# Input's block sums moved to VectorE and ScalarE, and the sample's new memory computed in the memory's stretch

## The chip, the cores and the metric

One core of one Trainium2 chip. The time is device microseconds of one execution. In what follows PE is TensorE (matmul), PEld its weight loads, DVE is VectorE, ACT is ScalarE, POOL is GpSimd, and SP issues most transfers.

## What is computed

One step of a hybrid encoder layer for 512 frames of a new stream and 32 frames of a running one (T = 544 columns in all, feature rows on the partitions). The input is normalised and projected; then come an mLSTM branch with four heads of 512 and an HGRN2 branch with eight heads of 128, a gated merge and an output block. The part that matters here is the projection and the mLSTM of one head:

```python
xn = _rmsnorm(h, norm_g[l])
proj = xn @ w_in[l]
c = silu(causal_conv(u))
q, k = ch @ w_qm, ch @ w_km * M_HD**-0.5
s = einsum('bhtd,bhsd->bhts', q, k) * dmat
num = w_inter * einsum('bhed,bhtd->bhte', C, q) + einsum('bhts,bhse->bhte', s, v)
den = w_inter * einsum('bhd,bhtd->bht', n, q) + s.sum(-1)
h = num / maximum(abs(den), exp(-m_t))
C_new = decay * C + einsum('bhs,bhse,bhsd->bhed', w_last, v, k)
```

`C_new` is wanted for both streams: the prompt's memory starts from zero, the sample's from a given state.

## The kernel before

Matmuls in full precision are built from two roundings: each operand is a high part (a cast) and a low part (the operand less its high part), and three products are added. Names end in `h` and `l` for the two, and `split_piece` and `weight` (recorded at L128 and L129) make them for weights, the cast on ACT and the subtraction on DVE or POOL. A dense product runs over two column halves of 272.

The order on PE, DVE and ACT is partly written by hand and partly by a scheduler. Start: squares of the input (`r0q`) are added and summed for the norm (`r0pc`, L215), while PE runs the first products `u`; then gates, the four value products `v` (`values`, `values_out` copies them out as `vt`), convolution and SiLU (`cv`, `c`, `cs`). Then for each mLSTM head h: `stage_k` (L149, `k`), `stage_q` in two halves (`q`), for head 0 between them `stage_cols` (gate rows to columns, `cols`) and `stage_decay` (`dm`, from a row `bc` that comes by DMA), `stage_scores` (`sc`, then `dm` times scores, `sh` and `sl`), `mchain`, and `stage_br` (`ya`).

`mchain` is a generator. It transposes and weighs keys (`kt`, then `kwh` on ACT and `kwl` on DVE, L870 and L871; for the sample `kts`, `kws`), transposes values (`vt`, `vh`, `vl`; for the sample `vts`, `vs`), builds the prompt's new memory (`memory`, `C`, `Co`), the numerators with the old state (`nm`, `y`), their statistics (`numbers`), the normalisation (`rs`), the sample's new memory (`Cs`, the last part before `yt`), and after a distance of at least GAP steps the transposes `yt`. Each `yield n` lets a `Pump` run n steps of other work on PE: the remaining projections. These come as `One` (a plain product) or `Two`, which makes two 512-column pieces with seven block products instead of eight (L466 `d`), from sums of weight blocks (`ws`, `wa`) and sums of Input's blocks. PSUM has two double buffers, tag `a` (`paux`), and a ring of four single ones, tag `h` (`phalves` takes two). A `One` or a `Two` holds two of the ring for as long as it runs.

Input's block sums are `xf`. Input has eight row tiles, `xh`/`xl` of 128 x 544. For each pair (k, k + 4) `xf_blocks` adds high and low part into `xr`, and `xf_sums` forms four combinations of the 272-column blocks and splits each into `xfh`, `xfl`. All of it is on POOL, issued in head 0 behind the copy `ksm` (k = 0 to 2) and behind `vsm`. The first `Two` that reads `xfh` is in head 0's `mchain`. POOL is also the engine that makes the first head's key weights' low parts and the copies `r` of gate rows (L692).

The call at the end of `stage_q(0, 1)`, as it stands, and the four calls in `mchain`:

```python
with tc.issue_after(st8[0]["copied"].ins):
    xf_blocks(0)
    xf_sums(0)
    xf_blocks(1)
    xf_blocks(2)
```

Of the kernel before, what the change touches and what calls it, by code (L numbers as in the profile page):

```python
# [33 lines left out]
LEVELS = (1, 2, 4, 8, 16, 32, 64)  # L34
GAP = 16
STEPS = (2, 3, 3, 3, 3, 3, 3)
# [17 lines left out]
WSPLIT = 256  # L54
U5, U7, U6, U4 = range(4)
TAIL = (5, 4)
# [6 lines left out]
def hybrid_step(ctx: ExitStack, tc: tile.TileContext, a, o):  # L63
# [238 lines left out]
    one, other = half(0), half(1)  # L302
    xraw = {}

    def xf_blocks(k):

        if k < KD // 2 - 1:
            t = xp.tile([P, 2 * T], F32, tag="x0", name=f"xr{k}")
            x = t[:, :T], t[:, T:]
        else:  # L310
            x = slot(f"xr{k}0")[:, :T], slot(f"xr{k}1")[:, :T]
        for t, i in zip(x, (k, k + KD // 2)):
            G.tensor_tensor(t, xs[i][0].bitcast(F32), xs[i][1].bitcast(F32), ALU.add)
        xraw[k] = x

    def xf_sums(k):

        x1, x2 = xraw[k]
        u = cp.tile([P, T], F32, tag="lm", name=f"xu{k}")
        u5, u7 = u[:, :TH], u[:, TH:T]  # L320
# [4 lines left out]
        def part_of(src, n):  # L325
            G.tensor_copy(h[:, n], src)
            G.tensor_tensor(l[:, n], src, h[:, n].bitcast(F32), ALU.subtract)

        G.tensor_tensor(u5, x1[:, one], x1[:, other], ALU.subtract)
        part_of(u5, U5)  # L330
        G.tensor_tensor(u7, x2[:, other], x1[:, other], ALU.subtract)
        part_of(u7, U7)
        G.tensor_tensor(x1[:, one], x1[:, one], x2[:, other], ALU.add)
        G.tensor_tensor(x2[:, other], x1[:, other], x1[:, one], ALU.subtract)
        G.tensor_tensor(x1[:, other], x1[:, other], x2[:, one], ALU.add)
        G.tensor_tensor(x2[:, one], x1[:, one], x1[:, other], ALU.subtract)
        part_of(x2[:, one], U4)
        part_of(x2[:, other], U6)
        xf.append((h, l))

    xf = []

# [373 lines left out]
    def stage_decay(h):  # L716

        bc = tp.tile([P, T + NS], F32, tag="bc", name=f"bc{h}")
        nc.sync.dma_start(bc, nm_d[h : h + 1, :].to_broadcast([P, T + NS]))
        d01 = [slot(f"dm{h}0"), slot(f"dm{h}1")]  # L720
        d2 = slot(f"dm{h}2")
        dj = [d01[0][:, 0:512], d01[1][:, 0:384], d2[:, 0:256], d2[:, 256:384]]
        ds = d2[: 3 * NS, 384 : 384 + NS]
        for j in range(NB):
            V.tensor_tensor(dj[j][:, :P], bc[:, NS + j * P : NS + (j + 1) * P], cmask, ALU.add)
# [6 lines left out]
        S.activation(ds, ds, AF.Exp, bias=cols[:, 0, h : h + 1])  # L732
        wi = cp.tile([P, NS], F32, name=f"wi{h}")
        G.tensor_copy(wi, bc[:, T : T + NS])
        st8[h].update(dj=dj, ds=ds, wi=wi)

# [51 lines left out]
    def stage_scores(h):  # L788
# [9 lines left out]
        for j in range(NB):  # L798
# [16 lines left out]
            S.copy(sh, dj[j])  # L815
            V.tensor_tensor(sl, dj[j], sh.bitcast(F32), ALU.subtract)
            st.append((sh, sl))
# [12 lines left out]
        V.tensor_tensor(dss[2 * NS :], ds[2 * NS :], dss[2 * NS :].bitcast(F32), ALU.subtract)  # L830
        st8[h].update(st=st, dss=dss)

    def memory(h, f, kw, vv, pool=paux):
# [23 lines left out]
    def mchain(h, pump):  # L857

        t = st8[h]

        kf, ksm = t["kf"], t["ksm"]
        kw = []
# [56 lines left out]
        lo = slice(NS, 2 * NS)  # L919
        V.tensor_tensor(vs[lo, :HD], pt[lo, 0, :], vs[lo, :HD].bitcast(F32), ALU.subtract)  # L920
# [20 lines left out]
        st, dss, qw, wi = (t[k] for k in ("st", "dss", "qw", "wi"))  # L941
        stt = small("stat", [P, NB + 1, 2])
# [42 lines left out]
        for i in range(NB):  # L985
# [15 lines left out]
            numbers(i, P, y)  # L1001
            yb.append(y)
        yb.append(ysm)
        n5 = NB + 1
        with tc.high_priority():
# [11 lines left out]
            for i in range(n5):  # L1017
# [4 lines left out]
                else:  # L1022
                    V.tensor_scalar(y, y, stt[:p, i, 0:1], rs[:p, i : i + 1], ALU.subtract, ALU.mult)

        for f in range(KH):
            yield 1
            pn = paux(f"Cs{h}{f}")
            for g in range(2):
                PE.matmul(
                    pn[:, g, :VH],  # L1030
                    kws[:, f * P : (f + 1) * P],
                    vs[:, g * VH : (g + 1) * VH],
                    start=True,
                    stop=True,
                )
            V.scalar_tensor_tensor(
                two(c0[f][:, :VW]), two(c0[f][:, :VW]), wi[:, NS - 1 : NS], pn[:, :, :VH], ALU.mult, ALU.add
            )
            nc.sync.dma_start(o["Cs"][h, f], c0[f][:, :VW])


# [18 lines left out]
    def stage_br(h):  # L1060

        hs = st8[h]["hs"]
        for u in range(4):
# [12 lines left out]
            if h + 1 < MH and len(st8[h + 1]["cc"]) < KH:  # L1076
                conv(h + 1)
        st8[h].clear()

    def level_masks():  # L1080
# [13 lines left out]
    with tc.manual_schedule(engines={mybir.EngineType.Activation, mybir.EngineType.DVE, mybir.EngineType.PE}):  # L1094
# [15 lines left out]
        for k in range(KD):  # L1110
# [10 lines left out]
            sqk = slot(f"r0q{k}")[:, :T]  # L1121
            if k in (1, 3, 5, 6, 7):
                S.activation(sqk, t[:, :T], AF.Square)
            else:
                G.tensor_tensor(sqk, t[:, :T], t[:, :T], ALU.mult)
            sq.append(sqk)
            if k in (1, 3, 5):
                G.tensor_tensor(sq[k - 1], sq[k - 1], sqk, ALU.add)
            if k > 1:
                products(k - 2)  # L1130
        for i, j in ((6, 7), (0, 2), (4, 6), (0, 4)):
            V.tensor_tensor(sq[i], sq[i], sq[j], ALU.add)
# [83 lines left out]

        values()
        conv_rest(0, uin[0], cv[0])
        silu()
        next(gates)  # L1220
        values_out()
        values()
        for f in range(1, KH):
            conv_rest(f, uin[f], cv[f])
            silu_low(f - 1)
            silu()
            if f == 1:
                values_out()
                values()
        values_out()  # L1230
        values()
        silu_low(KH - 1)
        for _ in range(GATED):
            next(gates)
    with tc.manual_schedule(engines={mybir.EngineType.PE}):
        for h in range(MH):
# [8 lines left out]
            if h == 0:  # L1245

                st8[0]["wq"] = weight(a["w_qm"][0, 0], "wq00")
                high, low = made["wq001"]
                with tc.issue_after(high.ins), tc.issue_after(low.ins):
                    *_, (nm_d, *rows) = gates  # L1250

                    lb, lc = cp.tile([P, HH], F32, name="lb"), cp.tile([P, HH], F32, name="lc")
                    l0, l1 = vec[:, V_LB : V_LB + HH], vec[:, V_LB + HH : V_LB + 2 * HH]
                    lm, le = small("lbm", [P, HH]), small("lbe", [P, 2, HH])
                    V.tensor_tensor(lm, l0, l1, ALU.max)
                    V.tensor_tensor(le[:, 0, :], l0, lm, ALU.subtract)
                    V.tensor_tensor(le[:, 1, :], l1, lm, ALU.subtract)
                    S.activation(le, le, AF.Exp)
                    V.tensor_tensor(lm, le[:, 0, :], le[:, 1, :], ALU.add)
                    V.reciprocal(lm, lm)  # L1260
                    V.tensor_tensor(lb, le[:, 0, :], lm, ALU.mult)
                    V.tensor_tensor(lc, le[:, 1, :], lm, ALU.mult)
            stage_q(h, 0)
            if h == 0:
                col, cols, combo = stage_cols(*rows)
                stage_decay(h)
            low = stage_q(h, 1)
            if h == 0:
                pump.behind = low
                with tc.issue_after(st8[0]["copied"].ins):  # L1270
                    xf_blocks(0)
                    xf_sums(0)
                    xf_blocks(1)
                    xf_blocks(2)
            else:
                pump = Pump(fill(h))
                pump.to(2)
            stage_scores(h)
            pump.run(mchain(h, pump))
            pump.end()  # L1280
            if h < MH - 1:
                stage_br(h)
            if h == 0:
                lmask = level_masks()
    nc.scalar.dma_start(o["u"], uo)
# [445 lines left out]
```

## Time and profile before

| | us |
|---|---|
| median of 3 runs | 1204.21 (1203.91 to 1205.76) |
| profiled execution | 1204.12 |
| its span | 1202.4 |
| mean granted PE clock | 0.989 |
| busy: PE, DVE, ACT, POOL | 1164.4, 887.8, 611.1, 188.0 |

Two views carry most of what follows. A row of the waits gives the waiting engine, tile and line, what it waited for, the total, the number of times and the longest. A row of a timeline gives start, duration, engine, line, operation, tiles and sizes, and in brackets the idle time before and what ended it; x2 means two instructions in one row, and the duration is then that of both. A line number such as L149 or L129 is that of a helper that many stages use, so the tiles tell which stage it is.

### The profile page before, as it was taken

What the parts mean: (1) busy time and instruction counts of PE and PEld (TensorE: products, weight loads), DVE (VectorE), ACT (ScalarE), POOL (GpSimd) and SP (SyncE); (2) the same over time, 40 slices, a digit from 0 to 9 for tenths busy, and PEclk for the clock granted to TensorE, in tenths of its full rate; (3) what the DMA queues carried; (4) which work ended last, traced back from release to release, by engine and by line L of the source; (5) the groups of instructions that cost most, each with busy time, mean ns of one, the idle gap of its engine ahead of it and who ended that gap; (6) DMA issues with size and microseconds to landing.
All of it is one profiled execution on the core that took longest, in us unless ns stands there. A gap on an engine that the chain in (4) does not pass through costs nothing.

```text
span 1202.4 us, 24275 instructions
## 1 busy us (share of the span) xinstructions
PE 1164.4 (97%) x9089; PEld 1133.9 (94%) x9089; DVE 887.8 (74%) x2099; ACT 611.1 (51%) x1344; POOL 188.0 (16%) x349
## 2 busy tenths in 40 slices
PE   9986898999999999999999999999999999999998
PEld 8985888999989999899999999999999999999998
DVE  7876768568598685986887577777778998654485
ACT  5673435746465564665564244434334566533462
POOL 5938541010010110001100011110011100000000
PEclk9996999999999999999999999999999999999999
DMA  6132211513255132552556321212222263322653
GB/s 225 55 101 78 71 71 61 182 53 133 80 155 187 54 116 84 164 176 73 183 173 209 108 69 60 69 62 69 67 62 77 67 219 96 120 89 84 222 183 111
DMA packets 77902, 135.82 MB, mean 113 GB/s; under 512 B 8788, under 2 KB 16340, under 8 KB 77784
## 3 DMA queue, kind: packets, MB, share of 16 engines
q1 hardware_dynamic: 77616, 134.21, 34.3%
q8 instruction: 71, 1.16, 0.4%
q14 instruction: 47, 0.39, 0.1%
q10 hardware_dynamic: 168, 0.06, 0.0%
HBM read 109.32 MB, written 24.91 MB: 112 GB/s over the span
## 4 chain that ended last, share of the span: by engine, by line
PE 85%; DVE 6%; ACT 3%; POOL 3%; issue 2%; DMA 0%; SPq 0%; ACTq 0%; DVEq 0%; POOLq 0%
PE d L466 21%; PE d L379 17%; PE ya L149 8%; PE pg L1590 4%; PE yb L149 4%; PE o L149 4%; PE k L149 4%; PE C L840 4%; PE q L149 4%; PE sc L803 2%; PE pl L1386 2%; PE nm L992 2%; DVE cv L580 1%; PE u L269 1%; PE ple L149 1%
## 5 line engine op out<-in xcount | busy, mean ns | idle before, releaser
L1378 ACT COPY km<-hk 128x256 f32<-128x256 f32 x56 | 24.0, 428 | 81.9 <-DVE hk L1404 61.1
L580 DVE SCALAR_TENSOR_TENSOR cv<-ub,vec,cv 128x547 f32<-128x547 f32 x48 | 40.1, 835 | 0.5
L1440 POOL TENSOR_TENSOR at<-at,tri 32x32 f32<-32x32 f32 x8 | 3.8, 472 | 208.7 <-DVE at L1411 208.7
L1386 PE MATMUL pl<-hq,km 128*128 128x128 f32 x224 | 35.9, 284 | 0.0
L892 DVE TENSOR_TENSOR c0l<-c,c0h 128x516 fp32r<-128x516 f32 x16 | 13.3, 852 | 26.2 <-ACT c0h L891 26.1
L1404 DVE TENSOR_TENSOR hq<-hq,q 128x128 f32<-128x128 f32 (+1 forms) x96 | 25.3, 294 | 9.7 <-PE pl L1386 8.4
L479 ACT COPY t<-d 128x272 f32<-128x272 f32 x78 | 29.4, 377 | 2.9 <-DVE ub L487 2.6
L1386 PEld LDWEIGHTS pl<-hq,km 128*128 128x128 f32 x224 | 30.8, 191 | 0.0
L851 ACT COPY Co<-C 128x258 f32<-128x258 f32 x32 | 10.4, 378 | 33.6 <-PE C L840 33.6
L1404 DVE TENSOR_TENSOR hk<-hk,q 128x128 f32<-128x128 f32 x96 | 26.2, 286 | 0.2
L1409 DVE COPY_PREDICATED at<-lmask,pl 128x256 f32<-128x256 uint8 x56 | 24.8, 443 | 0.0
L1074 DVE TENSOR_TENSOR y<-ya,y 128x272 f32<-128x272 f32 x48 | 18.9, 435 | 7.9 <-PE ya L149 7.9
L1328 POOL TENSOR_TENSOR kq<-q,hk 128x544 f32<-128x544 f32 x8 | 13.9, 1733 | 60.5 <-DVE q L1326 57.6
L1500 ACT ACTIVATE osq<-kq 128x128 f32<-128x128 f32 x32 | 9.9, 311 | 25.5 <-DVE kq L1494 24.8
L953 DVE BATCH_NORM_STATS2 bs<-y 128x6 f32<-128x512 f32 (+1 forms) x20 | 13.7, 685 | 10.9 <-ACT y L1000 10.8
L742 POOL COPY vsm<-vt 128x96 f32<-128x96 f32 x16 | 7.6, 483 | 87.1 <-ACT vt L489 43.6
L573 POOL COPY uo<-ub 128x3 f32<-128x3 f32 x16 | 9.2, 573 | 71.7 <-DVE ub L485 37.8
L1000 ACT COPY y<-nm 128x516 f32<-128x516 f32 x16 | 9.4, 589 | 20.5 <-PE nm L992 14.8
L840 PE MATMUL C<-vh,kwh 128*128 128x258 f32 x96 | 19.4, 284 | 0.0
L840 PE MATMUL C<-vl,kwh 128*128 128x258 f32 x96 | 19.4, 284 | 0.0
L840 PE MATMUL C<-vh,kwl 128*128 128x258 f32 x96 | 19.3, 283 | 0.0
L992 PE MATMUL nm<-vh,sh 128*128 128x258 f32 x80 | 16.5, 288 | 2.7 <-ACT y L1000 2.5
(4087 smaller groups left out, 4925.9 us busy)
## 6 DMA issues: line engine op xcount, KB each, us to landing
ya_d<-y SPq DMA_DIRECT2D x32, 272.0 KB, 2.4
y<-ya_d SPq DMA_DIRECT2D x24, 272.0 KB, 4.3
c<-in_C SPq DMA_DIRECT2D x16, 258.0 KB, 3.4
out_Cp<-Co SPq DMA_DIRECT2D x16, 258.0 KB, 2.4
out_Cs<-c SPq DMA_DIRECT2D x16, 258.0 KB, 2.8
x<-in_xT SPq DMA_DIRECT2D x8, 272.5 KB, 4.7
ya<-ya_d SPq DMA_DIRECT2D x8, 272.0 KB, 5.1
h<-in_xT SPq DMA_DIRECT2D x8, 272.0 KB, 3.7
```

The costliest lines, as they stand in the source:

```text
L149: PE.matmul(both[b][:m, :TH], part(w, off + k * step, m, x), xx[:, half(b)], start=(k == 0 and j == 0), stop=(k == n - 1 and j == 2),)
L379: PE.matmul(self.ps[b][:, : c.stop - c.start], part(self.w, k * P, P, x), xx[:, c], start=(k == 0 and j == 0), stop=(k == KD - 1 and j == 2),)
L466: PE.matmul(ps, ww[:, c], xx, start=(start and k == 0 and j == 0), stop=end, skip_group_check=not start,)
L479: S.copy(t, ps)
L580: V.scalar_tensor_tensor(cv[:, :547], ub[:, j : j + 547], vcol(V_CW + 4 * ft + j), cv[:, :547], ALU.mult, ALU.add)
L803: PE.matmul(pn[:, 0, :n], ks[f][x][:, j * P : (j + 1) * P], qs[f][y][:, NS + j * P : T], start=(f == 0 and i == 0), stop=(f == KH - 1 and ...
L840: PE.matmul(pn[g][:, :VH], kw[b][x][:, f * P : (f + 1) * P], vv[b][y][:, g * VH : (g + 1) * VH], start=(b == 0 and j == 0), stop=(b == NB ...
L992: PE.matmul(pn[:, g, :VH], st[j][x][:, (i - j) * P : (i - j + 1) * P], vv[j][y][:, g * VH : (g + 1) * VH], start=(j == 0 and q == 0), stop ...
L1386: PE.matmul(pn[:, 0, b * P : (b + 1) * P], km[:, b * P : (b + 1) * P], view(qq, b * P, ((2 * c, P // (2 * c)), (HB + c, 2), (1, c))), star ...
L1404: V.tensor_tensor(xv[:, :, i, :], xv[:, :, i, :], t[:, :, 1 - i : 2 - i].to_broadcast([P, m, c]), ALU.mult)
L1409: V.copy_predicated(at[:, :NA], lmask[:, li, :NA], pn[:, 0, :NA])
L1590: PE.matmul(ps, part(w, k * P, P, x), xx[:, c], start=(k == 0 and j == 0), stop=(k == KD - 1 and j == 2))
```

## The change

Block sums. `xf_blocks` is gone. `xf_sums` does ten operations on DVE and three on ACT: it adds high and low part (544 columns for the first tile, two halves for the second), forms the four combinations in place with four more, casts on ACT and subtracts on DVE. Two of the combinations are cast and split together as 544 columns; the fourth comes out with its sign changed, which the multiplication by −1 undoes. k = 0 and 3 are issued behind the last low part of the scores, k = 1 and 2 behind the low part of `vs`. U4 and U6, which number the combinations, swap places. Scratch is the `lm` tile and the three `half` tiles that `Two` uses as well.

The sample's memory. `new_memory(f)` replaces the last loop before `yt`. It takes single halves of the ring instead of a double buffer, so that DVE has two additions of 258 columns per f instead of one of 516. It is called behind `memory(f)` for f = 0, 1 and behind the numerators 1 and 2 for f = 2, 3; in the last head behind each numerator. The loop's four `yield 1` go, and GAP is 20 instead of 16, so `yt` stands at the same distance.

Smaller parts: the level masks are issued behind the last weight split of `stage_br(0)`; HGRN2's lower bounds are computed in three places (start, behind the decays, behind the scores); the gate rows' POOL and DVE work is bound behind `wk011`'s low part; ACT squares all input tiles but two, and DVE adds two pairs early and three at the end; `values` and `values_out` are issued earlier.

```diff
-GAP = 16
+GAP = 20
-U5, U7, U6, U4 = range(4)
+U5, U7, U4, U6 = range(4)
...
     def xf_sums(k):
...
+        x11, x12 = u[:, one], u[:, other]
+        x21, x22 = (tp.tile([P, TH], F32, tag="half", name=f"xv{k}{b}", bufs=3) for b in range(2))
+        (h1, l1), (h2, l2) = ([t.bitcast(F32) for t in xs[i]] for i in (k, k + KD // 2))
+        V.tensor_tensor(u, h1, l1, ALU.add)
+        for b, t in enumerate((x21, x22)):
+            V.tensor_tensor(t, h2[:, half(b)], l2[:, half(b)], ALU.add)
+        V.tensor_tensor(x11, x11, x12, ALU.subtract)
+        V.tensor_tensor(x12, x22, x12, ALU.subtract)
+        V.tensor_tensor(x22, x11, x22, ALU.add)
+        V.tensor_tensor(x21, x22, x21, ALU.subtract)
+        S.copy(h[:, :2], two(u))
+        V.tensor_tensor(l[:, :2], two(u), h[:, :2].bitcast(F32), ALU.subtract)
+        S.copy(h[:, 2], x21)
+        V.tensor_tensor(l[:, 2], x21, h[:, 2].bitcast(F32), ALU.subtract)
+        S.mul(h[:, 3], x22, -1.0)
+        V.scalar_tensor_tensor(l[:, 3], x22, -1.0, h[:, 3].bitcast(F32), ALU.mult, ALU.subtract)
+        return h, l
...
         if h == 0:
-            with tc.issue_after(copied.ins):
-                xf_sums(1)
-                xf_sums(2)
-                xf_blocks(3)
-                xf_sums(3)
+            with tc.issue_after(low.ins):
+                for k in (1, 2):
+                    xf[k] = xf_sums(k)
...
+        def new_memory(f):
+
+            pn = phalves(f"Cs{h}{f}")
+            for g in range(2):
+                v = slice(g * VH, (g + 1) * VH)
+                PE.matmul(pn[g][:, :VH], kws[:, f * P : (f + 1) * P], vs[:, v], start=True, stop=True)
+                V.scalar_tensor_tensor(c0[f][:, v], c0[f][:, v], wi[:, NS - 1 : NS], pn[g][:, :VH], ALU.mult, ALU.add)
+            nc.sync.dma_start(o["Cs"][h, f], c0[f][:, :VW])
...
                 for _ in memory(h, f, kw, vv):
                     pass
+                if f < 2:
+                    new_memory(f)
...
             yb.append(y)
+            if h == MH - 1:
+                new_memory(i)
+            elif i in (1, 2):
+                new_memory(i + 1)
...
-        for f in range(KH):
-            yield 1
-            pn = paux(f"Cs{h}{f}")
...
-            if k in (1, 3, 5, 6, 7):
+            if k not in (0, 2):
                 S.activation(sqk, t[:, :T], AF.Square)
...
-            if k in (1, 3, 5):
+            if k in (1, 3):
                 G.tensor_tensor(sq[k - 1], sq[k - 1], sqk, ALU.add)
+            if k in (5, 6):
+                i, j = ((0, 2), (4, 5))[k - 5]
+                V.tensor_tensor(sq[i], sq[i], sq[j], ALU.add)
...
-        for i, j in ((6, 7), (0, 2), (4, 6), (0, 4)):
+        for i, j in ((0, 4), (6, 7), (0, 6)):
...
-                high, low = made["wq001"]
-                with tc.issue_after(high.ins), tc.issue_after(low.ins):
+                with tc.issue_after(made["wq001"][0].ins), tc.issue_after(made["wk011"][1].ins):
                     *_, (nm_d, *rows) = gates
...
-                with tc.issue_after(st8[0]["copied"].ins):
-                    xf_blocks(0)
...
-            stage_scores(h)
+            low = stage_scores(h)
+            if h == 0:
+                with tc.issue_after(low.ins):
+                    for k in (0, 3):
+                        xf[k] = xf_sums(k)
+                    lower_bounds()
...
             if h == 0:
-                lmask = level_masks()
+                with tc.issue_after(last.ins):
+                    lmask = level_masks()
```

How the order of instructions moves, at three places (numbers behind tile names are buffer numbers). First, DVE in head 0's q stage, before and then after; `wq010l` and `wq011l` are the low parts of the second query weight, `dm` the start of the decay matrices, line 725 before and 712 after.

```order
L707 COPY col<-cols 128x72
L709 COPY cols<-cols 96x12
L129 TENSOR_TENSOR wq010l<-wq01r_1398,wq010h 128x512
L725 TENSOR_TENSOR dm_1377<-bc_1375,cmask 128x128
L725 TENSOR_TENSOR dm_1378<-bc_1375,cmask 128x128
L725 TENSOR_TENSOR dm_1379<-bc_1375,cmask 128x128 x2
L726 TENSOR_TENSOR dm_1379<-bc_1375,cmask_128 96x32
L129 TENSOR_TENSOR wq011l<-wq01r_1400,wq011h 128x512
```

```order
L694 COPY col<-cols 128x72
L696 COPY cols<-cols 96x12
L129 TENSOR_TENSOR wq010l<-wq01r_1394,wq010h 128x512
L129 TENSOR_TENSOR wq011l<-wq01r_1396,wq011h 128x512
L712 TENSOR_TENSOR dm_1367<-bc_1365,cmask 128x128
```

The second low part has moved ahead of the five `dm` operations; on POOL the operations of the sums that stood between the last `ksm` copy and the `vsm` copies are gone, and so are those behind them. Second, DVE in head 0 behind the scores, after the change: `xu` and `xv` are scratch of the sums, `xfl` their low parts, `lbm`, `lb`, `lc` the lower bounds. These are the first of the four `kwl` and the rows behind it.

```order
L859 SCALAR_TENSOR_TENSOR kwl_1621<-kt_1615,col,kwh_1620 128x512
L318 TENSOR_TENSOR xv_1571<-xu_1569,xv_1571 128x272
L1080 RECIPROCAL lbm<-lbm 128x8
L319 TENSOR_TENSOR xv_1570<-xv_1571,xv_1570 128x272
L321 TENSOR_TENSOR xfl_1568<-xu_1569,xfh_1567 128x544
L323 TENSOR_TENSOR xfl_1568<-xv_1570,xfh_1567 128x272
L325 SCALAR_TENSOR_TENSOR xfl_1568<-xv_1571,xfh_1567 128x272
L313 TENSOR_TENSOR xu_1587<-xh_604,xl_605 128x544
L315 TENSOR_TENSOR xv_1589<-xh_628,xl_629 128x272
L316 TENSOR_TENSOR xu_1587<-xu_1587 128x272
L1081 TENSOR_TENSOR lb<-lbe,lbm 128x8
L1082 TENSOR_TENSOR lc<-lbe,lbm 128x8
```

One more operation of the sums (L317) and then the second `kwl` follow. Before, these two `kwl` stood next to each other (L871). Ahead of the first `kwl` now stand six operations of the sums (L313 to L317) that before were on POOL. Third, PE in head 1, around the sample's memory of f = 0, after the change: `C` is the prompt's memory, `Cs` the sample's.

```order
L828 MATMUL C_3968<-vh_3879,kwl_3645 128x258 x2
L921 MATMUL Cs_3997<-vs,kws 128x258
L921 MATMUL Cs_3998<-vs,kws 128x258
L828 MATMUL C_4004<-vh_3821,kwh_3492 128x258 x2
L828 MATMUL C_4004<-vl_3822,kwh_3492 128x258 x2
```

Before, `C` of f = 0 was followed at once by `C` of f = 1, and the four pairs of `Cs` came behind all numerators with six matmuls of `d` between two pairs. The second `Cs` here takes the one half of the ring that the first has left to DVE.

More of the change, by code (lines that the diff above doesn't have):

```diff
@@ L302, in hybrid_step @@
     one, other = half(0), half(1)
[L303 to L314, printed above, removed]
     def xf_sums(k):
-        x1, x2 = xraw[k]
-        u = cp.tile([P, T], F32, tag="lm", name=f"xu{k}")
-        u5, u7 = u[:, :TH], u[:, TH:T]
         ring = f"x{int(k in (1, 2))}"
@@ L323, in xf_sums @@
         l = xp.tile([P, 4, TH], F32R, tag=ring, name=f"xfl{k}")
[L325 to L341, printed above, removed]
+        u = cp.tile([P, T], F32, tag="lm", name=f"xu{k}")
+        x11, x12 = u[:, one], u[:, other]
[15 more added lines that the diff above has]
+        return h, l
+    xf = [None] * (KD // 2)
     class One:
@@ L815, in stage_scores @@
             S.copy(sh, dj[j])
-            V.tensor_tensor(sl, dj[j], sh.bitcast(F32), ALU.subtract)
+            low = V.tensor_tensor(sl, dj[j], sh.bitcast(F32), ALU.subtract)
             st.append((sh, sl))
@@ L831, in stage_scores @@
         st8[h].update(st=st, dss=dss)
+        return low
     def memory(h, f, kw, vv, pool=paux):
@@ L859, in mchain @@
         t = st8[h]
-        kf, ksm = t["kf"], t["ksm"]
+        kf, ksm, wi = t["kf"], t["ksm"], t["wi"]
         kw = []
@@ L938, in mchain @@
                     pass
-        st, dss, qw, wi = (t[k] for k in ("st", "dss", "qw", "wi"))
+                if f < 2:
+                    new_memory(f)
+        st, dss, qw = (t[k] for k in ("st", "dss", "qw"))
         stt = small("stat", [P, NB + 1, 2])
@@ L1023, in mchain @@
                     V.tensor_scalar(y, y, stt[:p, i, 0:1], rs[:p, i : i + 1], ALU.subtract, ALU.mult)
-        for f in range(KH):
-            yield 1
-            pn = paux(f"Cs{h}{f}")
[L1028 to L1039, printed above, removed]
         hs = []
@@ L1078, in stage_br, with hgrn_bounds, rest @@
         st8[h].clear()
+        return made[f"wbm{h}31"][1]
+    lb, lc = cp.tile([P, HH], F32, name="lb"), cp.tile([P, HH], F32, name="lc")
+    def hgrn_bounds(decayed):
+        l0, l1 = vec[:, V_LB : V_LB + HH], vec[:, V_LB + HH : V_LB + 2 * HH]
+        lm, le = small("lbm", [P, HH]), small("lbe", [P, 2, HH])
+        V.tensor_tensor(lm, l0, l1, ALU.max)
+        V.tensor_tensor(le[:, 0, :], l0, lm, ALU.subtract)
+        V.tensor_tensor(le[:, 1, :], l1, lm, ALU.subtract)
+        with tc.issue_after(decayed.ins):
+            S.activation(le, le, AF.Exp)
+        def rest():
+            V.tensor_tensor(lm, le[:, 0, :], le[:, 1, :], ALU.add)
+            V.reciprocal(lm, lm)
+            V.tensor_tensor(lb, le[:, 0, :], lm, ALU.mult)
+            V.tensor_tensor(lc, le[:, 1, :], lm, ALU.mult)
+        return rest
     def level_masks():
@@ L1217, in hybrid_step @@
         values()
+        values_out()
+        values()
         conv_rest(0, uin[0], cv[0])
@@ L1225, in hybrid_step @@
             silu_low(f - 1)
+            if f == KH - 1:
+                values_out()
+                values()
             silu()
@@ L1281, in hybrid_step @@
             if h < MH - 1:
-                stage_br(h)
+                last = stage_br(h)
             if h == 0:
-                lmask = level_masks()
+                with tc.issue_after(last.ins):
+                    lmask = level_masks()
     nc.scalar.dma_start(o["u"], uo)
```

25 lines of the change are left out of this document (4 added, 21 removed).

## The prediction

> **What bounds the kernel now.** I read the busy times first, then the whole list of what TensorE waited for, then the stretches in which it waits. The page's busy row of each engine:
>
> ```profile
> span 1202.4 us, 24275 instructions
> PE 1164.4 (97%) x9089; PEld 1133.9 (94%) x9089; DVE 887.8 (74%) x2099; ACT 611.1 (51%) x1344; POOL 188.0 (16%) x349
> ```
>
> TensorE (PE) is the bound: 38.0 us of the span are not matmul, and only those, and matmuls that run slowly, can be won. The profiled execution took 1204.12 us, 1.7 us more than its span, and agrees with the median of 1204.21 us, so I work from 1204.1. The view of PE's waits (total us, times, longest) has nearly all of the 38 us; these are the rows that the change can touch:
>
> ```profile
> PE d L466 <- DVE ub L485: 6.0, 3, 3.0
> PE q L149 <- DVE wq010l L129: 5.4, 1, 5.4
> PE q L149 <- DVE wq011l L129: 4.7, 1, 4.7
> PE nm L992 <- ACT y L1000: 2.5, 1, 2.5
> PE vts L915 <- POOL vh L908: 2.0, 1, 2.0
> PE cols L705 <- POOL r L692: 1.9, 1, 1.9
> PE k L149 <- POOL wk001l L129: 1.7, 1, 1.7
> PE d L379 <- ACT vt L1201: 1.5, 1, 1.5
> PE r0pc L215 <- DVE r0q L1132: 1.3, 1, 1.3
> PE d L466 <- ACT t L479: 1.2, 1, 1.2
> PE kt L867 <- DVE dm L810: 1.2, 1, 1.2
> PE v L149 <- DVE vt L1203: 1.0, 1, 1.0
> PE Cs L1029 <- DVE c L1036: 0.3, 1, 0.3
> ```
>
> Two of them, in head 0's q stage, are 10.1 us. The table by stretches shows what goes on there (columns: length, then busy us of PE, PEld, DVE, ACT and POOL with counts, then the granted PE clock):
>
> ```profile
> 20.00:30.00 10.00, 8.72 (x58) 8.38 (x57) 6.72 (x27) 1.48 (x6) 0.00 (x0) 0.83 0.32 106
> 90.00:100.00 10.00, 7.66 (x64) 7.09 (x63) 5.04 (x12) 6.17 (x21) 9.98 (x15) 0.86 0.47 155
> 100.00:110.00 10.00, 3.09 (x12) 2.76 (x12) 10.00 (x4) 1.57 (x5) 10.00 (x16) 0.50 0.08 26
> 110.00:120.00 10.00, 7.24 (x36) 7.07 (x37) 4.33 (x10) 3.55 (x12) 6.50 (x18) 0.61 0.16 58
> 280.00:320.00 40.00, 39.95 (x328) 39.51 (x327) 25.96 (x47) 20.15 (x43) 2.13 (x9) 1.00 0.31 107
> ```
>
> From 100 to 110 DVE began only 4 instructions, with POOL busy without a gap, and PE's clock was 0.50. The timelines of DVE and POOL have the instructions (start, duration):
>
> ```profile
> 98.66 6.32 DVE L129 TENSOR_TENSOR wq010l<-wq01r,wq010h 128x512 fp32r<-128x512 f32 x1
> 104.90 6.55 DVE L725 TENSOR_TENSOR dm<-bc,cmask 128x128 f32<-128x128 f32 x4
> 112.03 0.68 DVE L129 TENSOR_TENSOR wq011l<-wq01r,wq011h 128x512 fp32r<-128x512 f32 x1
> ```
>
> ```profile
> 100.00 1.32 POOL L313 TENSOR_TENSOR xr<-xh,xl 128x544 f32<-128x544 f32 x1
> ```
>
> The same operation took 6.32 us in one place and 0.68 us, once POOL was quieter, 13 us later. POOL was doing Input's block sums there (`xr`, `xu`, `xfh`, `xfl`), which began behind the `ksm` copies. [...]
>
> **The change, part by part.**
>
> *The q stage: about −15.7 us.* These are PE's rows at the stage's start, its last pair of matmuls, and the first of the scores behind it:
>
> ```profile
> 98.07 0.32 PE L705 MATMUL cols<-ident,r 4*96 4x4 f32 x2 [1.94 <-POOL r L692]
> 118.83 0.42 PE L149 MATMUL q<-cs3h,wq011l 128*128 128x272 f32 x2
> 119.08 0.63 PE L803 MATMUL sc<-q,kh 128*128 128x512 f32 x2
> ```
>
> From 98.32 to 119.08 are 20.76 us for 48 matmuls. Two take 0.25 us (118.83 to 119.08), so 6.0 us would do; 5.4 and 4.7 us are the two waits, and the remaining 4.7 us is a slow clock (0.50 and 0.61 in the table). In the new order POOL has no sums there, `r` no longer stands behind any, and DVE makes `wq010l` and `wq011l` one behind the other, ahead of `dm`. PE gets `cols` 1.94 us sooner; then DVE copies `cols` (0.3 us) and makes `wq010l` (0.68), while PE needs that after its first four matmuls (0.5): 0.5 us of waiting is left, and `wq011l` is ready before its turn. Gain 1.94 + 5.4 + 4.7 + 4.7 − 0.5 = 16.2; I take 15.7, leaving 0.5 for matmuls that still run slowly after the small `cols` ones. Bounds: 12.5 (3 us of slow clock stay) to 16.5. The scores need `q`'s low parts and `dm`, each then short on a free DVE: nothing later there that I can find.
>
> *From the start to k: about −4.5 us.* Gone are the wait at `r0pc` (1.3; three additions of squares at the end instead of four, and no POOL squares beside DVE), at `v` (1.0) and `vt` (1.5), since `values_out` is issued earlier, and at `wk001l` (1.7, as POOL no longer copies `r` first): 5.5 us. The clock of 0.83 from 20 to 30, 10 × 0.17 = 1.7 us, may go with the first. What is late next is ScalarE's cast of the first key weight, with POOL's low part behind it:
>
> ```profile
> 72.99 0.61 ACT L128 CAST wk000h<-wk00r 128x512 fp32r<-128x512 f32 x1
> 73.67 1.32 POOL L129 TENSOR_TENSOR wk000l<-wk00r,wk000h 128x512 fp32r<-128x512 f32 x1 [12.51 <-ACT wk000h L128]
> 74.63 0.41 PE L149 MATMUL k<-cs0h,wk000h 128*128 128x272 f32 x2
> ```
>
> The cast ended 1.0 us before PE used it, and now two `vt` copies (0.6 us) stand ahead of it. The chain before it (convolution, SiLU, two function tables) moves forward too, by the shift at `rb` and by two DVE operations fewer ahead of the last convolution, but not by all of PE's 5 us. I charge 2.5 us at `wk000h` and `wk000l`: 5.5 + 1.7 − 2.5 = 4.7, rounded to 4.5. Bounds: 2.0 to 7.2.
>
> *Head 0 from scores to normalise: about +1.1 us.* Gone: `kt` 1.2, `vts` 2.0, `nm` 2.5, `t` 1.2 and `Cs` 0.3, all with POOL's sums at their source: 7.2. New: the sums of k = 0 and 3 stand in DVE's queue before and between the four `kwl`. The prices of their operations, and of `kwl`, from rows on a DVE that was not held up:
>
> ```profile
> 120.05 0.79 DVE L780 TENSOR_TENSOR q<-q,q 128x272 fp32r<-128x272 f32 x2 [4.00 <-ACT q L779]
> 130.92 0.75 DVE L871 SCALAR_TENSOR_TENSOR kwl<-kt,col,kwh 128x512 fp32r<-128x512 f32 x1
> 192.87 0.73 DVE L102 TENSOR_TENSOR hm0l<-c,hm0h 128x544 fp32r<-128x544 f32 x1
> ```
>
> One sum has two operations of 0.73 and eight of 0.40 us, 4.7 us. PE's transposes `kt` have two buffers, each freed by a `kwl`, and between two of them PE has about 1.2 us of other work. Six operations stand ahead of the first `kwl`, 0.73 + 5 × 0.40 = 2.7 us: a wait of 1.5. Nine and three tiny ones of the bounds stand ahead of the second; DVE starts them closer than they last, so about 4.0 us, and with `kwl` itself, less PE's work, a wait of 3.5. What stands before the third and fourth makes `vt` wait 0.8 and `vts` 1.2. Together 7.0, and a slow clock behind the longest. That one I price by a wait of the same length:
>
> ```profile
> 203.57 0.59 PE L466 MATMUL d<-xfh,ws16h 128*128 128x272 f32 x1 [2.99 <-DVE ub L485]
> 203.96 0.43 PE L466 MATMUL d<-xfl,ws16h 128*128 128x272 f32 x1
> ```
>
> The 12 matmuls behind it took 0.23 us each instead of 0.125: 1.3 us. The sums of k = 1 and 2 (9.4 us of DVE) lie beside the memory's matmuls and are not needed until `d` some 20 us later; I cost them at nothing. Without that cover they would cost up to 9.4 us. Sum: 7.0 + 1.3 − 7.2 = +1.1. Bounds: −3 (ScalarE's copies of the sums let `kwl` pass sooner) to +10.
>
> *The sample's memory, heads 1 to 3: about +7.8 us.* `Cs` now takes single halves of PSUM. In head 0 two halves are free. From head 1 on two seven-product units hold three of four, so the second half's matmul waits until DVE has added the first from PSUM. No row of before has this wait; its parts have:
>
> ```profile
> 172.47 0.75 DVE L1036 SCALAR_TENSOR_TENSOR c<-c,wi,Cs 128x516 f32<-128x516 f32 x1
> 173.27 0.51 PE L1029 MATMUL Cs<-vs,kws 96*128 96x258 f32 x2 [0.26 <-DVE c L1036]
> 189.53 0.43 DVE L487 SCALAR_TENSOR_TENSOR ub<-d,t 128x272 f32<-128x272 f32 x1
> 200.30 0.29 PE L466 MATMUL d<-xfh,ws36l 128*128 128x272 f32 x1
> ```
>
> The matmul takes 0.29 us to its end, the addition of 258 columns about 0.43, and PE went on 0.05 us after such a release (172.47 + 0.75 = 173.22, start 173.27); less the 0.12 us that it would have run anyhow, 0.65 us. Four f in three heads make 12 such waits: 7.8 us. Bounds: 0.35 us each, 4 us (if the rows overstate the matmul's end), to 1.2 each, 14 us (one `BATCH_NORM_STATS` or split of 0.7 us ahead on DVE). DVE is busy 25.96 of 40 us in the head's quiet part (280 to 320). Behind each addition on DVE wait only splits for later units.
>
> *Heads 1 and 2 behind the normalise: about −2.4 us.* Two of the three `ub` waits (1.5 each) are theirs. In the new order DVE has two splits (0.6 each) behind it before `yt` that stood after it, so I take 1.2 off each; bounds 0 and 3.6. Head 0's wait of 3.0 with its slow clock I leave, since the order there is the same. The lower bounds, the level masks (now where DVE has room) and the swapped order of two blocks I cost at 0 within ±1.
>
> Sum: −15.7 − 4.5 + 1.1 + 7.8 − 2.4 = −13.7, so **1190 us**.
>
> **The rivals.**
>
> *DVE becomes the bound of head 0.* All four sums add 18.8 us to DVE from 120 to 165. For it: they are 18.8 us more in 45 us where it already waits in line. Against: most of them have PE work beside them. If k = 1 and 2 are not hidden, 9.4 us come on top: about 1199.
>
> *The long `ub` wait goes too.* With 3.0 + 1.3 us in head 0, the rest of the 3.6 in heads 1 and 2, and the start at its best: 1190 − 4.3 − 1.2 − 2 = about 1183. For it: the masks and additions leave DVE ahead of that wait. Against: its chain starts at `yt`.
>
> *The hand-over in halves eats everything.* All else gives 21.5 us (13.7 + 7.8), so 12 hand-overs must cost over 1.8 us each to make the kernel slower. That needs three operations ahead of each addition on DVE; the 3.0 us of `ub` shows PE held by such a queue, and at 3.0 each the time is 1204.1 − 21.5 + 36 = 1219. Against: the additions stand next to each other in the new order, with DVE a third idle.
>
> *The hand-over lowers the clock.* If each short gap brought the 1.3 us of slow matmuls seen after 203.57, that is 15.6 us more: about 1205, no change. Against: after waits of 1.0 and 1.5 us (`v`, `vt`) no slow stretch follows. [...]
>
> That POOL's sums did not hold up DVE at all, and 6.32 us came from elsewhere, I give no chance of its own: it would leave the q stage as it is.
>
> **How the numbers follow.** Forecast 1190: 0.60; DVE bound in head 0, 1199: 0.16; `ub` wait gone, 1183: 0.14; clock, 1205: 0.04; slow hand-over, 1219: 0.06. A measurement of this kernel tells about 0.2%, 2.4 us, from no change. So faster 0.90, same 0.04, slower 0.06. The range 1181 to 1200 holds the first three and leaves out the last two with the tails of the others.
>
> **What would show it.** Right: `wq010l` at 0.7 us, the clock at 1.00 between 90 and 110, and in the waits a row of `Cs` on DVE with 12 times and about 8 us; in head 0 a row of `kt` on `kwl` of about 5 us. Wrong: `Cs` waits over 1 us each, a lower clock in the memory's stretches, waits of `d` on `xfl`, or a k stage that starts no earlier.

## The result, and the profile after

| | before | after |
|---|---|---|
| median of 17 runs each, us | 1203.12 (1201.25 to 1205.76) | 1200.46 (1197.59 to 1204.94) |
| ratio, 95% interval | | 0.9981 [0.9971, 0.9991] |
| profiled execution, us | 1204.12 | 1202.97 |

2.7 us came of a forecast 13.7. The profiled execution of after is 2.5 us above its median. First the page's busy row, then the waits of PE:

```profile
span 1201.3 us, 24295 instructions
PE 1170.1 (97%) x9089; PEld 1138.1 (95%) x9089; DVE 885.6 (74%) x2156; ACT 615.7 (51%) x1357; POOL 133.7 (11%) x283
```

```profile
PE Cs L921 <- DVE c L922: 8.9, 12, 2.6
PE kt L855 <- DVE kwl L859: 4.8, 2, 3.3
PE d L453 <- DVE ub L472: 3.1, 1, 3.1
PE d L453 <- ACT wbm101h L128: 1.6, 1, 1.6
PE d L453 <- ACT wbm201h L128: 1.6, 1, 1.6
PE v L149 <- ACT vt L1210: 1.5, 1, 1.5
PE k L149 <- POOL wk000l L129: 1.3, 1, 1.3
PE vts L903 <- DVE vl L895: 1.1, 1, 1.1
PE q L149 <- DVE wq010l L129: 0.3, 1, 0.3
```

Span less PE's busy time fell from 38.0 to 31.2 us, 6.8 us, but PE was busy 5.7 us longer with as many matmuls. The mean clock hardly differs (0.991 against 0.989), but before's longest slow stretch lay beside waits (100 to 120), while those of after lie where PE works. The q stage's 10.1 us of waits are down to 0.3; the `Cs` row has the forecast 12 times. The table by stretches (columns as in the prediction):

```profile
20.00:30.00 10.00, 9.62 (x76) 9.10 (x75) 6.71 (x29) 2.53 (x10) 0.57 (x1) 1.00 0.33 114
60.00:80.00 20.00, 18.51 (x133) 18.06 (x133) 17.01 (x29) 14.68 (x28) 5.31 (x4) 0.91 0.34 105
90.00:100.00 10.00, 9.70 (x87) 9.32 (x86) 5.23 (x18) 7.51 (x27) 2.06 (x9) 1.00 0.51 165
100.00:110.00 10.00, 10.00 (x71) 9.45 (x71) 8.30 (x17) 5.32 (x12) 3.44 (x10) 1.00 0.36 111
280.00:320.00 40.00, 37.67 (x299) 36.46 (x298) 24.94 (x71) 19.43 (x41) 1.26 (x9) 1.00 0.25 84
600.00:620.00 20.00, 18.21 (x120) 17.38 (x121) 10.94 (x40) 6.50 (x12) 0.00 (x0) 0.83 0.16 59
```

From 90 to 110 the clock is full, as forecast. From 280 to 320, in head 1's memory, PE is idle 2.3 us at a full clock: four hand-overs (the matmul of one half, its addition on DVE, then the matmul that reuses the half). From 600 to 620, in the last head's memory, the clock is 0.83: 20 × 0.17 = 3.4 us. PE's timeline shows a hand-over in head 1 and the first in the last head:

```profile
286.93 0.28 PE L921 MATMUL Cs<-vs,kws 96*128 96x258 f32 x1
287.79 0.39 PE L921 MATMUL Cs<-vs,kws 96*128 96x258 f32 x1 [0.58 <-DVE c L922]
...
597.18 0.28 PE L921 MATMUL Cs<-vs,kws 96*128 96x258 f32 x1
600.06 0.39 PE L921 MATMUL Cs<-vs,kws 96*128 96x258 f32 x1 [2.60 <-DVE c L922]
...
601.23 0.63 PE L990 MATMUL nm<-vh,sh 128*128 128x258 f32 x2
601.66 0.63 PE L990 MATMUL nm<-vl,sh 128*128 128x258 f32 x2
...
610.93 0.40 PE L990 MATMUL nm<-vh,sh 128*128 128x258 f32 x2
611.17 0.40 PE L990 MATMUL nm<-vl,sh 128*128 128x258 f32 x2
```

The second matmul starts 0.86 us behind the first in head 1, 0.74 more than the 0.12 without a wait. Eleven of the twelve waits are such ones of 0.58. The twelfth is 2.60, and behind it a pair of matmuls takes 0.43 us instead of 0.24 until 607.3. DVE's timeline shows why:

```profile
597.67 0.68 DVE L129 TENSOR_TENSOR ws346l<-ws,ws346h 128x512 fp32r<-128x512 f32 x1
598.27 0.69 DVE L880 TENSOR_TENSOR c0l<-c,c0h 128x516 fp32r<-128x516 f32 x1
598.87 0.69 DVE L951 BATCH_NORM_STATS2 bs<-y 128x6 f32<-128x512 f32 x1
599.48 0.14 DVE L953 COPY den<-y 128x1 f32<-128x1 f32 x1
599.53 0.47 DVE L922 SCALAR_TENSOR_TENSOR c<-c,wi,Cs 128x258 f32<-128x258 f32 x1
```

The first matmul of the two ended at 597.46, and four operations stood ahead of its addition.

### The profile page after: what moved, and what is told of

Read it like the earlier page. It is cut to its first block, busy times and chain, and to the rows that moved or that the text cites. A ratio compares the mean times of both kernels' runs of the same rounds, so it can differ in the third digit from the quotient of the medians.

```text
span 1201.3 us, 24295 instructions
## 1 busy us (share of the span) xinstructions
PE 1170.1 (97%) x9089; PEld 1138.1 (95%) x9089; DVE 885.6 (74%) x2156; ACT 615.7 (51%) x1357; POOL 133.7 (11%) x283
## 5 line engine op out<-in xcount | busy, mean ns | idle before, releaser
L922 DVE SCALAR_TENSOR_TENSOR c<-c,wi,Cs 128x258 f32<-128x258 f32 x32 | 15.2, 480 | 19.1 <-PE Cs L921 19.0
L921 PE MATMUL Cs<-vs,kws 96*128 96x258 f32 x32 | 10.2, 336 | 8.9 <-DVE c L922 8.9
L742 ACT ACTIVATE kf<-k 128x272 f32<-128x272 f32 x32 | 10.9, 392 | 14.6 <-PE k L149 14.6
L573 ACT ACTIVATE c<-cv 128x32 f32<-128x32 f32 x16 | 3.7, 230 | 27.8 <-DVE cv L567 27.8
```

## The experiments

**Theory A** after the result: the block sums brought what was forecast, and the hand-over took it back, much of it in the last head. **Theory C**, for the rest: the start brought 1 to 2.5 us, not 4.5.

**The sample's memory back as it was** (after, with before's loop over `f` and its GAP):

```diff
-GAP = 20
+GAP = 16
...
-                if f < 2:
-                    new_memory(f)
...
-            if h == MH - 1:
-                new_memory(i)
-            elif i in (1, 2):
-                new_memory(i + 1)
...
+        for f in range(KH):
+            yield 1
+            pn = paux(f"Cs{h}{f}")
...
```

> The changed kernel with the sample's memory put back where it was (a double buffer per f, behind the normalise, distance 16); all else as changed. Theory A (the hand-over of single halves, with what follows it, costs some 14 us in heads 1 to 3: 12 waits of 0.58 or more, the late first one in the last head, and the slow clock behind two of them): about 1188, 12 us under the changed kernel, no row of Cs on DVE over 0.3 us in the waits. Rival B (the gain of head 0 is lost again to a clock that falls somewhere else whenever a wait goes, whatever is done with the sample's memory): within 3 us of the changed kernel, 1198 to 1203.

1188.14 us against 1203.94 of before on that chip, ratio 0.9869 [0.9854, 0.9884]. So all the rest of the change brings 15.8 us, and the sample's memory in its new place costs 1200.46 − 1188.14 = 12.3. Its waits have no row of `Cs`. The three `ub` waits stay:

```profile
PE d L453 <- DVE ub L472: 6.1, 3, 3.1
PE kt L855 <- DVE kwl L859: 4.8, 2, 3.3
```

**The sample's memory alone, on before** (GAP 20, `new_memory` and its calls; nothing else of the change):

> The kernel before with the sample's memory alone moved and cut into halves, as in the change. Theory A: 10 to 15 us slower than before, 1213 to 1218, with 12 waits of Cs on DVE, about 9 us, and the rest as slow clock and matmul tails. Rival B: within 3 us of before.

1220.95 us, ratio 1.0146 [1.0121, 1.017]: 17 us slower than before, more than expected and more than the 12.3 it costs in after. Two waits more than in after, in head 0 (5.4 and 0.5 us), are somewhat more than the difference of 4.7; the row of the waits, then DVE's timeline before the longest:

```profile
PE Cs L935 <- DVE c L936: 14.8, 14, 5.4
```

```profile
163.25 0.83 DVE L1083 TENSOR_SCALAR lmask<-sxt 128x256 uint8<-128x256 f32 x1 [2.84 <-POOL xfl L327]
...
168.01 0.47 DVE L936 SCALAR_TENSOR_TENSOR c<-c,wi,Cs 128x258 f32<-128x258 f32 x1
```

The level masks, which reuse a buffer of POOL's block sums, wait for these at 163.25 and stand ahead of the addition until 168.01. In after they are elsewhere, and head 0 has no such wait: the parts of the change lean on each other.

**Block sums alone, on before** (the new `xf_sums`, its calls and the order of U4 and U6):

> The kernel before with the block sums alone moved to VectorE and ScalarE. If it is POOL's sums that held DVE up in the q stage: wq010l at 0.7 us instead of 6.32, and 11 to 15 us faster than before (1188 to 1192), a little less than with wq011l moved ahead of dm as well, and the waits of kt on kwl of about 5 us appear. Rival (the order of wq011l behind dm, or the r copies, carry most of the q stage): under 6 us faster, wq011l or cols still waited for 3 us or more.

1189.26 us, ratio 0.9878 [0.9863, 0.9892]: 1203.94 − 1189.26 = 14.7 us. `wq010l` lasts 0.68 us, and PE waits 0.3 for it and 0.8 for `wq011l`. For `kwl` it waits 1.5 at `kt` and 2.1 at `kts`, 3.6 of the expected 5.

**The start alone, on before**:

```diff
-            if k in (1, 3, 5, 6, 7):
+            if k not in (0, 2):
                 S.activation(sqk, t[:, :T], AF.Square)
...
+            if f == KH - 1:
+                values_out()
+                values()
...
-                with tc.issue_after(high.ins), tc.issue_after(low.ins):
+                with tc.issue_after(made["wq001"][0].ins), tc.issue_after(made["wk011"][1].ins):
```

> The kernel before with the start alone as in the change: squares on ACT and DVE, values issued earlier, the gate rows' copies behind the last key weight. As predicted this part gains 4.5 us; theory C, from the traces of the two versions that differ by it (q begins 2.3 us earlier, and the waits of v on vt 1.5 and of k on wk000l 1.3 take the place of three old ones): 1 to 2.5 us under before. Rival: nothing, within 1 us.

1202.58 us against 1203.79, ratio 0.9988 [0.9979, 0.9997]: 1.2 us. Theory C holds. In after, ACT, POOL and PE show one of the waits that it brings, at the next operand's chain:

```profile
71.47 0.61 ACT L128 CAST wk000h<-wk00r 128x512 fp32r<-128x512 f32 x1
```

```profile
72.16 1.98 POOL L129 TENSOR_TENSOR wk000l<-wk00r,wk000h 128x512 fp32r<-128x512 f32 x1 [13.24 <-ACT wk000h L128]
```

```profile
74.19 0.52 PE L149 MATMUL k<-cs0h,wk000l 128*128 128x272 f32 x2 [1.28 <-POOL wk000l L129]
```

The cast is 1.52 us earlier than in before (72.99), but POOL's low part took 1.98 instead of 1.32 us, beside a scan of DVE that had begun before it (L645, at 71.80), and ended only 0.85 us earlier (74.14 against 74.99). PE waits for it.

**The last head's part put back** (after, with before's loop in head 3 alone and its distance to `yt` 16 there):

> The changed kernel with the sample's memory put back in the last head alone; heads 0 to 2 as changed. It splits the 12 to 14 us. Theory A1 (most of it is the last head, where the first addition stands behind DVE's backlog and the matmuls after it run slowly: 8 us in the trace; heads 1 and 2 cost 3 us each): 1192 to 1194, 8 waits of Cs of 0.58 us left, no slow clock from 600 to 620. Rival A2 (the 12 hand-overs share it evenly, a third each): 1196 to 1197.

1192.18 us, ratio 0.991 [0.9896, 0.9924]: 8.3 of the 12.3 us lie in the last head, 4.0 in heads 0 to 2 together. The executions spread by 3.4 us, but the profiles agree: from the first `ya` of head 2 to that of the last head they have 137.5 us in after and 129.0 here. With that part back, PE has no gap in the last head's stretch and a full clock:

```profile
600.00:640.00 40.00, 40.00 (x317) 38.88 (x316) 32.07 (x85) 23.87 (x44) 1.76 (x1) 1.00 0.40 129
```

**Halves set apart** (after; in heads 0 to 2 the eight halves come one at a time, each behind at least six matmuls, twelve in head 1's trace, and the last head is as before):

```diff
-        def new_memory(f):
+        def new_half(f, g):
-            pn = phalves(f"Cs{h}{f}")
-            for g in range(2):
+            pn = pd.tile([P, 512], F32, tag="h", name=f"Cs{h}{f}{g}")
...
-                for _ in memory(h, f, kw, vv):
-                    pass
-                if f < 2:
-                    new_memory(f)
+                for n, _ in enumerate(memory(h, f, kw, vv)):
+                    at = {(0, 3): (0, 0), (1, 1): (0, 1), (1, 3): (1, 0), (2, 1): (1, 1)}.get((f, n))
+                    if at:
+                        new_half(*at)
```

> The changed kernel with the eight halves of the sample's memory set apart: in heads 0 to 2 one half at a time behind pieces of the prompt's memory and of the numerators, six or more matmuls between two halves, and in the last head as before the change. Theory A: the waits of Cs on DVE go to under 0.5 us in all, and the time is that of the version with the memory put back, about 1188. Rival (what costs is not the wait but DVE's 24 additions there, in halves, ahead of other work): the waits go, but others on DVE take their place, and the time stays above 1194.

1186.81 us, ratio 0.9853 [0.9833, 0.9873]; no row of `Cs` is left. So in heads 1 and 2 it was the second half's place right behind the first that cost, not the halves: the same matmuls and additions, with work in between, wait for nothing. For the last head, where the old loop is back, this run does not show it.

**And all sums behind `vs`** (the kernel of the last run, with the sums of k = 0 and 3 issued there too):

```diff
-                for k in (1, 2):
+                for k in range(KD // 2):
...
-                    for k in (0, 3):
-                        xf[k] = xf_sums(k)
```

> The version with the halves set apart, and with all four block sums behind the values of the sample instead of two of them behind the scores. If the sums' place ahead of kwl costs what the trace of the changed kernel has (kt 4.8 us of waits and a slow clock of 1.3 behind the longer one): 4 to 6 us under the version with the halves set apart, about 1181, no wait of kt on kwl. Rival (DVE becomes the bound later in head 0, and the sums' 18.8 us delay the additions of Cs, the statistics or d): waits of 3 us or more on Cs, nm or d in head 0 take the place, and the time stays within 2 us of 1187.

1183.13 us (1182.73 to 1183.42), ratio 0.9826 [0.9812, 0.9839], **the fastest median here**. The `kt` row is gone; one wait took its place, in head 0, where the sums are now ahead of an addition:

```profile
PE Cs L920 <- DVE c L921: 2.6, 1, 2.6
```

The medians of the two differ by 1186.81 − 1183.13 = 3.7 us, but the traces do not place them: the profiled executions took 1183.31 (halves set apart) and 1183.32. Here `vts` starts 6.6 us earlier (122.17 against 128.77), yet the first `ya` at the same time (189.71 and 189.73). The wait of 2.6 lies between, and so do two stretches of slower clock (0.91 from 130 to 150, 0.83 from 180 to 190) where the other profile has 1.00 (mean clock 0.997 and 0.998). The four executions here lie within 0.7 us, those with the halves set apart within 5.2.

**What held DVE in before?** Four kernels, one execution each (before took 1203.0 to 1204.4 beside them), add POOL operations whose result nobody reads to this last version, behind `ksm`, where before had the block sums. 14 additions of 128x544, all into one scratch tile:

```diff
+                junk = cp.tile([P, T], F32, tag="lm", name="junk")
+                with tc.issue_after(st8[0]["copied"].ins):
+                    for _ in range(14):
+                        G.tensor_tensor(junk, xs[0][0].bitcast(F32), xs[0][1].bitcast(F32), ALU.add)
```

> The version with all sums late, with 14 additions of 128x544 on POOL that nobody reads, issued where POOL's sums were (behind ksm); they are added work, the outputs stay. Theory S (POOL's two-input operations, back to back, keep DVE out until POOL stops): wq010l lasts as long as the rest of the additions, 5 to 9 us, PE waits for it that long, and the time is 8 us or more over 1183. [...]

1191.39 us, the 8 us over 1183 that theory S had. DVE and POOL:

```profile
95.50 1.28 DVE L129 TENSOR_TENSOR wq010l<-wq01r,wq010h 128x512 fp32r<-128x512 f32 x1
96.71 1.82 DVE L129 TENSOR_TENSOR wq011l<-wq01r,wq011h 128x512 fp32r<-128x512 f32 x1
```

```profile
94.90 15.88 POOL L1288 TENSOR_TENSOR junk<-xh,xl 128x544 f32<-128x544 f32 x10
```

DVE lost 0.6 and 1.1 us at these two operations (0.68 us each in the last run, without the additions), and the ten additions took 1.59 us each, where the first, at 88.14, took 1.36. So both went on, and the theory that DVE starves until POOL stops fell for this sequence. PE's wait for `wq010l` is only 0.9 us; the time lies in other waits (1.1 at `cols`, 1.2 at `sc`) and in the clock (0.992 against 0.997). Then 24 copies instead (`G.tensor_copy(junk, xs[0][0].bitcast(F32))`):

> The same with 24 copies of 128x544 instead of additions. Theory S with two-input operations alone at fault: wq010l stays near 0.7 us and no wait over 1 us comes of it. Rival (any busy POOL holds DVE up): wq010l over 3 us here too.

1186.27 us; a copy costs DVE less than an addition, not nothing:

```profile
95.17 1.10 DVE L129 TENSOR_TENSOR wq010l<-wq01r,wq010h 128x512 fp32r<-128x512 f32 x1
96.20 1.12 DVE L129 TENSOR_TENSOR wq011l<-wq01r,wq011h 128x512 fp32r<-128x512 f32 x1
```

Neither gave 6.32. In both, each operation writes the tile of the one before and has to wait for it (two of the copies in a row took 1.34 us at 91.04, one alone 0.64); in before, the additions for the next pair (L313) stood between the operations of the first, and from 97.99 to 105.8 each operation began 0.03 to 0.05 us before the end that its neighbour shows:

```profile
97.99 1.33 POOL L313 TENSOR_TENSOR xr<-xh,xl 128x544 f32<-128x544 f32 x1
99.28 0.75 POOL L334 TENSOR_TENSOR xr<-xr 128x272 f32<-128x272 f32 x1
...
101.28 0.74 POOL L335 TENSOR_TENSOR xr<-xr 128x272 f32<-128x272 f32 x1
```

So 28 additions of 272 columns, in turn into two halves of the tile:

```diff
+                    for i in range(28):
+                        hb = half(i % 2)
+                        G.tensor_tensor(junk[:, hb], xs[0][0].bitcast(F32)[:, hb], xs[0][1].bitcast(F32)[:, hb], ALU.add)
```

> The kernel of the run with all sums late, plus 28 unread POOL additions of 128x272 behind the copy `ksm`, written in turn to two halves of one scratch tile, so that none has to wait for the one before it. [...] Theory L (the turn passes after every POOL instruction, whatever follows): `wq010l` and `wq011l` last 1.0 to 1.6 us each, the time is 1185 to 1190, and before's 6.32 us stay unexplained by these runs.

1202.38 us against the 1185 to 1190 of theory L, nearly all the gain gone: PE waits 11.8 us for `wq010l`, and 2.9 at `cols` for a copy on POOL. DVE, then POOL:

```profile
98.32 12.18 DVE L129 TENSOR_TENSOR wq010l<-wq01r,wq010h 128x512 fp32r<-128x512 f32 x1
110.42 0.74 DVE L129 TENSOR_TENSOR wq011l<-wq01r,wq011h 128x512 fp32r<-128x512 f32 x1
```

```profile
97.72 12.17 POOL L1289 TENSOR_TENSOR junk<-xh,xl 128x272 f32<-128x272 f32 x17
109.85 1.98 POOL L729 COPY vsm<-vt 128x96 f32<-128x96 f32 x4
```

And the same 28 all into one half (`hb = half(0)`), which leaves size and number as they were:

> As the run with 28 additions in two halves in turn, which held `wq010l` for 12.18 us, but all 28 written to the same half, so that each waits for the one before. Theory N (what holds VectorE is that POOL's next instruction has nothing to wait for): `wq010l` and `wq011l` last 1.0 to 1.6 us each, no wait of PE on them over 1 us, time 1183 to 1190. Rival (the size of 272 columns, or the number of additions, made the difference to the 14 of 544): `wq010l` lasts 8 us or more again, time over 1195.

1191.03 us, 1 us over theory N's range, and `wq010l` is shorter than the 1.0 to 1.6 it gave, but the operations themselves decide against the rival's 8 us or more:

```profile
95.46 0.71 DVE L129 TENSOR_TENSOR wq010l<-wq01r,wq010h 128x512 fp32r<-128x512 f32 x1
96.08 1.25 DVE L129 TENSOR_TENSOR wq011l<-wq01r,wq011h 128x512 fp32r<-128x512 f32 x1
```

```profile
94.86 17.45 POOL L1289 TENSOR_TENSOR junk<-xh,xl 128x272 f32<-128x272 f32 x17
```

17 additions kept DVE out for their whole 12.17 us when none waited for its neighbour, and let it in between (17.45 us, `wq010l` 0.71) when each did. Theory N holds for these additions. That it is also the cause of before's 6.32 follows by likeness, the missing gaps on POOL included: the order of the block sums on POOL was not itself varied.

## Why the prediction was wrong, point by point

| term | forecast | measured |
|---|---|---|
| start to k | −4.5 | −2.4 up to q, −1.2 at the end (alone) |
| q stage and head 0 together | −14.6 | −14.7 (block sums alone) |
| sample's memory, hand-over of `Cs` | +7.8 | +12.3 (after less its undoing) |
| heads 1 and 2 behind the normalise | −2.4 | 0 (waits 3.0 before, 3.2 after) |
| sum | −13.7 | −3.6 (with −1.2); −2.7 as one |

- **The q stage was right**, mechanism and size: `wq010l` and `wq011l` take 0.68 each, PE waits 0.3, and from the first `cols` to the first `sc` it is 8.0 us instead of 24.3, 16.2 won for a forecast 15.7. I had gone by the trace's 6.32 and put the whole delay down to POOL's sums. The added POOL work shows a short delay and a long one: where POOL's additions followed one another by data, each of DVE's two low parts lost 1.1 us at most (1.82 against 0.68); where they did not, `wq010l` lost 11.5 (12.18 against 0.68) beside 17 of them.
- **The `kt` waits were right** (1.5 and 3.3 for the forecast 1.5 and 3.5), and so was head 0's sum: with the sample's memory put back, `sc` to `yt` takes 70.4 us against 69.1 before, +1.3 for +1.1. One term had the wrong source: the wait on `t` (1.2) stays with the sums moved (1.1 alone) and goes with the sample's memory (1.4 with it put back, 0.3 in after).
- **The step that failed most is "Four f in three heads make 12 such waits: 7.8 us".** The mechanism and the single price were right: 0.74 for a forecast 0.65, and from `ya` to `ya` head 1 takes 155.3 us in after and 152.7 with the part put back, 2.6 for four as forecast. But I priced the last head as one of three alike. There `new_memory` stands behind each numerator, and on DVE splits of the old state and the numerators' statistics stand ahead of the first addition: 2.6 us of waiting, some 3 us of slow clock behind it, and 8.3 instead of 2.6 in all. The rival had "three operations ahead" as its point of decision, and I dismissed it by the order of the additions and the quiet part of head 1, 280 to 320, which says nothing of the last head. The waits and the slow pairs of the profiled execution explain about 8 of the 8.3; how much the clock takes differs between executions (mean clock 0.997 at 1197.59 us, 0.990 at 1204.94).
- **The start was mis-sized.** The charge "2.5 us at `wk000h` and `wk000l`" covered what came there: the start alone has 0.3 and 1.3. But the sum had no term for three other waits that it has: `v` on `vt` 1.6, which moved to ACT's copy of `vt` instead of going, `u` on `x` 0.7, and `r0pb` 0.3. So 4.2 us of new waits stand against the 5.5 that went. With the faster clock of the start, the first matmul of `q` comes 2.4 us earlier (86.31 against 88.69). About half of that is left at the end; in head 0 its clock is 0.83 from 160 to 170, where before has 1.00 (mean clock 0.989 in both).
- **Heads 1 and 2 gained nothing.** The splits that moved were not what PE waited for. The two waits have another name now, `wbm101h` and `wbm201h` on ACT, but in after PE goes on at 343.03 right behind DVE's `ub`, as in before at 357.60. The cast `wbm101h` ends at the same moment (342.89) and is no operand of the matmul that waits:

```profile
342.48 0.40 DVE L472 TENSOR_TENSOR ub<-d,t 128x240 f32<-128x240 f32 x1
```

- **Of the signs named as wrong**, two came, each in one place: a `Cs` wait over 1 us and a lower clock in a memory stretch. The k stage starts 2.5 us earlier (72.14 against 74.63), but its third pair of matmuls, which needs `wk000l`, only 0.9 (74.19 against 75.13). No wait of `d` on `xfl` came, so DVE did not become the bound of head 0.
- **"The hand-over lowers the clock"** was right in the last head only. Eight waits of 0.58 us in heads 1 and 2 left the clock at 1.00 (280 to 320 and 440 to 460); the slow stretches of this profile stand behind single waits of 1.3 (`wk000l`), 1.6 (498 us), 2.6 (597 us), 3.1 (`ub`, 186 us) and 3.3 (`kt`).

## What to carry to other kernels

Price a new hand-over at each of its places from what stands ahead of it on the engine that frees the buffer: the same code cost 0.74 us at each place in head 1 and, with the slow clock behind one long wait, 8.3 in the last head. Two halves back to back in one buffer paid the way to the other engine and back each time, while halves with twelve matmuls between them paid nothing. When waits are taken away from PE's path, ask of each whether it goes or only moves, as `v` on `vt` did, and whether the next operand's own chain moves too.

## What the runs showed of the hardware

POOL additions without dependence on their neighbours kept DVE's `wq010l` out for 12.18 us, until the last of 17 was done; with dependence, a low part lost 0 to 1.1 us (0.71 to 1.82 against 0.68). POOL copies beside DVE cost it about 0.4 us per operation (1.10 against 0.68). It goes the other way too: POOL's `wk000l` (begun at 72.16 in after) took 1.98 us beside a scan of DVE that had begun at 71.80 and took 1.28. In before `wk000l` began first, at 73.67, and took 1.32, and the scan, begun at 73.86, took 2.27. In both, the one that began second lasted longer. What else in POOL's sequence lets DVE in was not tried. And a slow stretch can come behind a short wait in one execution and not in another: the clock of 0.91 from 60 to 80, behind a wait of 1.3 on `wk000l`, is in the profile of after, while the start alone has the same wait and 1.00 there.
